# GpSimd's two-tensor operations in pieces of 256 columns, and a modulation stage that starts nine feeds later

## The chip, the cores and the metric

The kernel runs on one core of a Trainium2 chip. The metric is the device time of one execution in microseconds (us), lower is better. TensorE (PE) multiplies, VectorE (DVE) and ScalarE (ACT) do elementwise work, GpSimd (POOL) does elementwise work in SBUF and issues the indirect DMAs, and SyncE (SP) issues nearly all other DMAs.

## The reference

The program computes three transformer layers on 1024 tokens of width 1024, in float32. What matters here is the first layer's modulation and attention, and the three output projections:

```python
mod = jax.nn.silu(c) @ w_ada[l] + b_ada[l]                 # 6 vectors of 1024
shift1, scale1, gate1, shift2, scale2, gate2 = jnp.split(mod, 6, axis=-1)
h = rms_norm(x, norm1_g[l]) * (1.0 + scale1) + shift1      # needs 2 of the 6
mla_out = mla_attention(...)                               # 4 heads, softmax
d_out = diff_attention(...)                                # 4 heads, softmax1 - lam * softmax2
d_out = rms_norm(d_out, subln_g[l]) * (1.0 - lambda_init)
mix = jnp.concatenate([mla_out, d_out], axis=-1) @ w_out[l]
x = x + gate1 * mix                                        # the other 4 come here and later
```

After it come a mixture of 32 experts, a layer with causal attention over 16 heads, and a layer with a window of 128 tokens over 16 heads; each of the two attention layers ends in an output projection of its own.

## The kernel before

The order of the work is written out by hand. Each engine runs its own instructions strictly in program order. The program order comes from generators: a unit of work is a Python generator, a `Pipe` (L70) holds the active ones, and each call of `go.feed` (L77) lets every active unit emit its instructions up to its next `yield`, in the order in which the units were added. One such call is a **feed**. A unit given to `spawn` begins with the next feed.

**Products in float32.** Every weight and activation is split into a high part and a rest (`split`, L332): the high part is a rounded copy, the rest is a subtraction. On the usual path ACT makes the copy and DVE the subtraction; with `e=G` GpSimd makes both (L338, L339) on tiles of 128x1024.

**Attention of the first layer** (`phase_attn`, L966) goes in 35 **rounds** of three feeds, counted from 0 (L1152): feed one adds a unit of the latent attention (`m_unit`, ten matmuls of 512 columns at L1079), feeds two and three add a unit of the differential attention each (`d_unit`, matmuls at L1116 and L1117, four of either a round). The latent units run three rounds behind (LAG = 3), so the first three rounds have no `m_unit`. In each round one `d_unit` ends on DVE with L1137 to L1140: L1138 is a tiny operation, L1139 adds the two softmax tiles of 128x1024, both with two inputs in SBUF, and TensorE's transposes at L1006 wait for L1139. Every second round a `d_end` (L1038) normalises one 256-column piece of the output: `rstd_of` (L319) is a DVE step (L321) and a power on GpSimd (L322); three feeds later L1054 and two L1056 on DVE use it, and TensorE's transposes at L1060 wait for these.

**The rest of the modulation** (`ada_rest`, L595) runs beside this attention, spawned just ahead of its first round (L1150). It goes 32 times over a piece of `w_ada`, 8 pieces for each of the four remaining vectors: SP loads the next piece (L581, 512 KB, a ring of two buffers, so the load waits until the sum that read the buffer is done), GpSimd scales the present one (L616) and adds it to the accumulator (L617), both 128x1024. The next iteration comes two or three feeds later, in turn. After eight, `finish` waits four feeds, lets TensorE sum over the partitions (L591), and SP writes the vector out (L608).

**Output weights** (`OutWeights`, L923): for the first layer GpSimd multiplies the four raw tiles of each half by the gate vector (`scale`, L932: four instructions of 128x1024) in rounds 30 and 34, and splits the first half in rounds 31 and 32 (`WO_ATTN`, L52, counted from `LAG`). The later layers give four and eight splits to GpSimd (`WO_FOX`, `WO_SWA`).

Of the kernel before, what the change touches and what calls it, by code (L numbers as in the profile page):

```python
# [14 lines left out]
OP = mybir.AluOpType  # L15
# [4 lines left out]
P = 128  # L20
S = 1024
D = 1024
# [13 lines left out]
LAG = 3  # L36
# [29 lines left out]
def f(ap):  # L66
    return ap.bitcast(F32)
# [226 lines left out]
def three_layer_kernel(ctx: ExitStack, tc: tile.TileContext, I, out, stop=99, dbg=None):  # L294
    nc = tc.nc
    V, A, G, T, SP = (GUARD(e) for e in (nc.vector, nc.scalar, nc.gpsimd, nc.tensor, nc.sync))
# [16 lines left out]
    def acopy(dst, src, scale=None):  # L313
        if scale is None:
            A.activation(out=dst, in_=src, func=AF.Copy)  # L315
        else:
            A.activation(out=dst, in_=src, func=AF.Copy, scale=scale)  # L317
# [10 lines left out]
    def bc_load(dst, src_row, n):  # L328
        SP.dma_start(out=dst, in_=bass.AP(tensor=src_row.tensor, offset=src_row.offset,
                                          ap=[[0, dst.shape[0]], [1, n]]))  # L330

    def split(hi, lo, src, scale=None, e=V):  # L332

        if scale is None:
            if e is V:
                A.activation(out=hi, in_=src, func=AF.Copy)  # L336
            else:
                e.tensor_copy(hi, src)  # L338
            e.tensor_tensor(lo, src, f(hi), op=OP.subtract)  # L339
        else:  # L340
            A.activation(out=hi, in_=src, func=AF.Copy, scale=scale)  # L341
            V.scalar_tensor_tensor(lo, src, scale, f(hi), op0=OP.mult, op1=OP.subtract)  # L342

    def split_k(hi, lo, raw, gain=None):
        if gain is None:
            split(hi, lo, raw)
        else:
            for k in range(raw.shape[1]):
                split(hi[:, k], lo[:, k], raw[:, k], gain[:, k:k + 1])
# [14 lines left out]
    def transposed(hi, lo, src, ps_ring=None, n=KD):  # L364

        m = src.shape[0]
        for c in range(0, n, 4):
            ps = (ps_ring or p_tr).tile([P, 4, P], name="tr")[:, :, :m]
            for k in range(4):
                T.transpose(ps[:, k], src[:, (c + k) * P:(c + k + 1) * P], ident[:m, :m])  # L370
            split(hi[:, c:c + 4], lo[:, c:c + 4], ps)
# [201 lines left out]
    def ada_acc(j, pl, e):  # L573
        acc = pl.tile([P, D], F32, name="acc", bufs=2)
        e.memset(acc, 0.0)
        SP.dma_start(out=acc[0:1], in_=I["b_ada"][0:1, j * D:(j + 1) * D])
        return acc

    def ada_load(pl, j, k):
        w = pl.tile([P, D], F32, name="adaw")  # L580
        SP.dma_start(out=w, in_=I["w_ada"][0][k * P:(k + 1) * P, j * D:(j + 1) * D])  # L581
        return w
# [4 lines left out]
    def ada_sum(acc, m=P):  # L587
        res = []
        for c in range(2):
            ps = p_tr.tile([P, 512], name="adaps")[0:m]  # L590
            T.matmul(ps, lhsT=ones[:, 0:m], rhs=acc[:, c * 512:(c + 1) * 512], start=True, stop=True)  # L591
            res.append(ps)
        return res

    def ada_rest():  # L595

        ad = Rings(sb, 2)
        todo = [(j, k) for j in range(2, 6) for k in range(KD)]
        w = ada_load(ad, *todo[0])
        accs = {}  # L600

        def finish(j):
            for _ in range(4):
                yield
            for c, ps in enumerate(ada_sum(accs[j], 1)):
                acopy(accs[j][0:1, c * 512:(c + 1) * 512], ps)
            yield
            SP.dma_start(out=d_mod[j:j + 1], in_=accs[j][0:1])  # L608
            if j == 5:
                ad.close()  # L610

        for i, (j, k) in enumerate(todo):
            w2 = ada_load(ad, *todo[i + 1]) if i + 1 < len(todo) else None
            if k == 0:
                accs[j] = ada_acc(j, ad, G)
            G.tensor_scalar(w, w, cc[:, k:k + 1], None, op0=OP.mult)  # L616
            G.tensor_tensor(accs[j], accs[j], w, op=OP.add)  # L617
            w = w2
            for _ in range(2 + i % 2):
                yield  # L620
            if k == KD - 1:
                go.spawn(finish(j))

# [299 lines left out]
    class OutWeights:  # L923
# [5 lines left out]
        def scale(self, c, row):  # L929

            for r in self.raw[c]:
                G.tensor_tensor(r, r, row[:, None, c * 512:(c + 1) * 512].to_broadcast([P, 2, 512]), op=OP.mult)  # L932

        def load(self, c):
            self.raw[c] = [sb.tile([P, 2, 512], F32, f"{self.name}{c}{q}") for q in range(4)]
# [30 lines left out]
    def phase_attn(wo, following):  # L966
# [181 lines left out]
        go.after(start_m)  # L1148
        go.feed()
        go.spawn(ada_rest())  # L1150
        seq = [(h, g, qi) for h in range(4) for g in range(4) for qi in range(2)]
        for i in range(len(seq) + LAG):  # L1152
# [1223 lines left out]
```

## Time and profile before

| | |
|---|---|
| Median of three runs | 2639.68 us |
| Lowest and highest | 2635.43 and 2639.68 us |
| Profiled execution | 2630.55 us |
| Its span, first to last instruction | 2628.8 us |
| Busy share: PE, DVE, ACT, POOL | 94%, 70%, 56%, 20% |
| Mean granted TensorE clock | 0.977 |

The profile comes from one execution of its own. An engine is busy when it executes; of DVE and GpSimd the time that an instruction waits for access to SBUF counts in its duration, so such a wait is seen as an instruction that takes longer than others of its kind. A time in brackets at a row's end is the idle time of the engine ahead of it, with what ended it.

### The profile page before, as it was taken

What the parts mean: (1) busy time and instruction counts of PE and PEld (TensorE: products, weight loads), DVE (VectorE), ACT (ScalarE), POOL (GpSimd) and SP (SyncE); (2) the same over time, 40 slices, a digit from 0 to 9 for tenths busy, and PEclk for the clock granted to TensorE, in tenths of its full rate; (3) what the DMA queues carried; (4) which work ended last, traced back from release to release, by engine and by line L of the source; (5) the groups of instructions that cost most, each with busy time, mean ns of one, the idle gap of its engine ahead of it and who ended that gap; (6) DMA issues with size and microseconds to landing.
All of it is one profiled execution on the core that took longest, in us unless ns stands there. A gap on an engine that the chain in (4) does not pass through costs nothing. (4 is left out here: it accounts for less than half of the span.)

```text
span 2628.8 us, 37168 instructions
## 1 busy us (share of the span) xinstructions
PE 2469.2 (94%) x13658; PEld 2057.6 (78%) x13658; DVE 1828.9 (70%) x3072; ACT 1460.3 (56%) x2557; POOL 529.2 (20%) x355
## 2 busy tenths in 40 slices
PE   5999899898997999999996999999999899999999
PEld 3789777776885777777765887898999789888877
DVE  7654589888667999999998444546888436735952
ACT  3325577676314888888874343446888224436830
POOL 0000276644101222222211012210002002300400
PEclk9999899999997999999998999999999999999999
DMA  7355865352766999999987534437667324337423
GB/s 264 113 143 157 248 199 156 127 156 99 236 223 211 387 387 390 385 379 378 384 300 265 179 112 124 139 105 189 175 167 207 115 87 147 120 108 184 142 70 107
DMA packets 270415, 530.04 MB, mean 202 GB/s; under 512 B 28027, under 2 KB 180603, under 8 KB 244118
## 3 DMA queue, kind: packets, MB, share of 16 engines
q1 hardware_dynamic: 263062, 510.84, 59.2%
q0 software_dynamic: 7168, 16.79, 1.9%
q8 instruction: 109, 1.79, 0.3%
q14 instruction: 76, 0.62, 0.1%
HBM read 424.19 MB, written 111.76 MB: 204 GB/s over the span
## 5 line engine op out<-in xcount | busy, mean ns | idle before, releaser
L358 PE MATMUL ps<-t,t 128*128 128x512 f32 (+5 forms) x8224 | 1760.3, 370 | 3.5 <-DVE t L339 2.6
L358 PEld LDWEIGHTS ps<-t,t 128*128 128x128 f32 (+1 forms) x8224 | 1379.0, 182 | 313.2 <-DVE t L339 4.9
L336 ACT ACTIVATE t<-ps 128x512 fp32r<-128x512 f32 (+3 forms) x660 | 334.8, 545 | 331.2 <-PE ps L370 204.6
L339 DVE TENSOR_TENSOR t<-t,t 128x2048 fp32r<-128x2048 f32 (+4 forms) x226 | 471.5, 2112 | 55.8 <-ACT t L336 55.7
L339 DVE TENSOR_TENSOR t<-ps,t 128x512 fp32r<-128x512 f32 (+3 forms) x660 | 392.1, 623 | 93.3 <-ACT t L336 86.5
L336 ACT ACTIVATE t<-t 128x2048 fp32r<-128x2048 f32 (+4 forms) x226 | 400.0, 1774 | 31.4 <-DVE t L764 10.9
L322 POOL TENSOR_TENSOR small<-small 128x8 f32<-128x8 f32 (+3 forms) x120 | 135.8, 1131 | 1006.9 <-DVE small L321 973.9
L317 ACT ACTIVATE t<-ps,small 96x512 f32<-96x512 f32 (+5 forms) x208 | 128.7, 619 | 335.1 <-PE ps L358 278.3
L315 ACT ACTIVATE t<-ps 128x256 f32<-128x256 f32 (+3 forms) x196 | 88.6, 454 | 133.5 <-PE ps L358 73.1
L370 PE MATMUL ps<-small,t 96*128 96x96 f32 (+1 forms) x736 | 96.0, 271 | 46.8 <-DMA t<-d_x 18.6
L370 PEld LDWEIGHTS ps<-small,t 96*128 96x128 f32 (+1 forms) x736 | 83.8, 147 | 67.6 <-DVE t L1869 19.0
L1501 POOL DMA_INDIRECT d_ye<-t,small x32 | 45.3, 1417 | 436.3 <-ACT t L317 429.7
L2036 DVE CUSTOM_DVE_ANT_0 t<-ps,t 128x1024 f32<-128x1024 f32 (+7 forms) x128 | 95.6, 747 | 20.0 <-PE ps L2031 18.1
L2118 DVE TENSOR_TENSOR t<-t,ps 128x512 f32<-128x512 f32 x32 | 22.0, 688 | 124.4 <-PE ps L358 124.4
L342 DVE SCALAR_TENSOR_TENSOR t<-t,small,t 128x512 fp32r<-128x512 f32 (+5 forms) x124 | 80.2, 692 | 36.1 <-ACT t L341 36.1
L616 POOL TENSOR_SCALAR t<-t,small 128x1024 f32<-128x1024 f32 x32 | 96.7, 3022 | 36.7 <-DMA t<-in_w_ada_dram 36.7
L2040 ACT ACTIVATE t<-t,small 128x1024 f32<-128x1024 f32 (+7 forms) x128 | 99.3, 776 | 7.3 <-DVE small L2036 5.3
L1497 POOL DMA_INDIRECT t<-d_h,small x32 | 89.0, 2781 | 33.7 <-DVE small L1205 24.3
L1698 DVE TENSOR_REDUCE small<-t 128x8 f32<-128x512 f32 (+1 forms) x56 | 36.2, 647 | 79.0 <-ACT t L1697 78.9
L1006 PE MATMUL ps<-small,t 128*128 128x128 f32 x512 | 69.8, 281 | 21.7 <-DVE t L1139 16.4
L1079 PE MATMUL ps<-t,t 128*128 128x512 f32 x320 | 83.8, 408 | 4.9 <-ACT t L1125 4.5
L2055 PE MATMUL ps<-small,t 128*128 128x128 f32 x576 | 85.4, 275 | 1.0 <-ACT t L2040 0.8
(298 smaller groups left out, 3070.3 us busy)
## 6 DMA issues: line engine op xcount, KB each, us to landing
t<-in_w_expert_gate_dram SPq DMA_DIRECT2D x64, 1024.0 KB
t<-in_w_expert_up_dram SPq DMA_DIRECT2D x64, 1024.0 KB
t<-in_w_expert_down_dram SPq DMA_DIRECT2D x64, 1024.0 KB
t<-in_w_ada_dram SPq DMA_DIRECT2D x48, 512.0 KB
t<-d_ak SPq DMA_DIRECT2D x64, 256.0 KB
t<-in_w_in_a_dram SPq DMA_DIRECT2D x12, 1024.0 KB
t<-in_x_dram SPq DMA_DIRECT2D x16, 512.0 KB
t<-d_dk SPq DMA_DIRECT2D x16, 512.0 KB
```

Source lines behind the costliest of these rows:

```text
L315: A.activation(out=dst, in_=src, func=AF.Copy)
L317: A.activation(out=dst, in_=src, func=AF.Copy, scale=scale)
L322: G.tensor_tensor(dst, dst, mhalf[:, :dst.shape[-1]], op=OP.pow)
L336: A.activation(out=hi, in_=src, func=AF.Copy)
L339: e.tensor_tensor(lo, src, f(hi), op=OP.subtract)
L358: T.matmul(ps, lhsT=a(k), rhs=b(k), start=(first and i == 0), stop=(last and i == n - 1))
L370: T.transpose(ps[:, k], src[:, (c + k) * P:(c + k + 1) * P], ident[:m, :m])
L616: G.tensor_scalar(w, w, cc[:, k:k + 1], None, op0=OP.mult)
L1497: G.indirect_dma_start(out=xg[e % 3], out_offset=None, in_=d_h2, in_offset=rows(idx_in[:CAP, e:e + 1]), bounds_check=S - 1, oob_is_err=False)
L2036: V.tensor_tensor_reduce(sbt[:, :n], ps[:, :n], c[:, :n], -1.0, 3e38, OP.add, OP.min, nm)
L2040: A.activation(out=pt[:, :n], in_=sbt[:, :n], func=AF.Exp, scale=-1.0, bias=nm, accum_out=RS[h][:, qt:qt + 1])
L2055: T.transpose(tr[:, j], pt[:, (b + j) * P:(b + j + 1) * P], ident)
```

## The change

A new helper `fine` issues a GpSimd two-tensor operation as pieces of 256 columns. Three places use it: the subtraction of `split` on GpSimd, the sum of `ada_rest`, and the product of `scale`. In `ada_rest` the first feeds change too: the first load is issued as before, both accumulators are reserved at once, and then nine feeds (3 * LAG) pass. In each iteration one feed now lies between scaling and sum, and one behind the sum, so an iteration takes two feeds instead of 2.5 on average. The sums are computed in the same order of pieces as before.

```diff
+    def fine(out, a, b, op):
+
+        for c in range(0, out.shape[-1], 256):
+            G.tensor_tensor(out[:, c:c + 256], a[:, c:c + 256], b[:, c:c + 256], op=op)
+
     def split(hi, lo, src, scale=None, e=V):
 
         if scale is None:
             if e is V:
                 A.activation(out=hi, in_=src, func=AF.Copy)
+                e.tensor_tensor(lo, src, f(hi), op=OP.subtract)
             else:
                 e.tensor_copy(hi, src)
-            e.tensor_tensor(lo, src, f(hi), op=OP.subtract)
+                for k in range(src.shape[1]):
+                    fine(lo[:, k], src[:, k], f(hi[:, k]), OP.subtract)
...
         w = ada_load(ad, *todo[0])
         accs = {}
+        ad.reserve("acc", D, 2)
+        for _ in range(3 * LAG):
+            yield
...
             G.tensor_scalar(w, w, cc[:, k:k + 1], None, op0=OP.mult)
-            G.tensor_tensor(accs[j], accs[j], w, op=OP.add)
+            yield
+            fine(accs[j], accs[j], w, OP.add)
             w = w2
-            for _ in range(2 + i % 2):
-                yield
+            yield
             if k == KD - 1:
                 go.spawn(finish(j))
...
             for r in self.raw[c]:
-                G.tensor_tensor(r, r, row[:, None, c * 512:(c + 1) * 512].to_broadcast([P, 2, 512]), op=OP.mult)
+                for k in range(2):
+                    fine(r[:, k], r[:, k], row[:, c * 512:(c + 1) * 512], OP.mult)
```

## Rows read from the trace of the kernel before

**Rows 1.** Page, part 1: engine, busy us, share of the span, instructions.
```profile
PE 2469.2 (94%) x13658; PEld 2057.6 (78%) x13658; DVE 1828.9 (70%) x3072; ACT 1460.3 (56%) x2557; POOL 529.2 (20%) x355
```
**Rows 2.** Stages: window, length, busy us (instructions) of PE, PEld, DVE, ACT, POOL; clock, DMA.
```profile
328.50:555.00 226.50, 203.27 (x1244) 173.27 (x1242) 200.54 (x291) 164.30 (x316) 153.32 (x67) 0.98 0.59 170
```
**Rows 3.** PE's waits, 328 to 570 us: who for whom, total us, times, longest.
```profile
PE ps L1006 <- DVE t L1139: 12.7, 9, 1.6
PE ps L1060 <- DVE t L1056: 5.5, 5, 1.5
...
PE ps L591 <- DVE t L339: 3.1, 1, 3.1
```
**Rows 4.** Two of DVE's lines over the span: duration ns min/median/max, first and last start.
```profile
L1139 DVE SCALAR_TENSOR_TENSOR t<-t,small,t x32: 1283/1285/3346, 317.5 to 654.0; 128x1024 f32<-128x1024 f32 x32
L1056 DVE TENSOR_SCALAR t<-t,small x32: 274/288/2477, 352.6 to 673.5; 128x128 f32<-128x128 f32 x32
```
**Rows 5.** DVE, in order of time: start us, duration us, instruction.
```profile
403.52 0.17 DVE L321 TENSOR_SCALAR small<-small 128x2 f32<-128x2 f32 x1 [1.14 <-ACT small L1048]
...
407.57 3.34 DVE L1139 SCALAR_TENSOR_TENSOR t<-t,small,t 128x1024 f32<-128x1024 f32 x1
...
413.49 0.15 DVE L1054 TENSOR_TENSOR small<-small 128x2 f32<-128x2 f32 x1
413.68 3.56 DVE L1056 TENSOR_SCALAR t<-t,small 128x128 f32<-128x128 f32 x2
```
**Rows 6.** POOL in order of time, the same stretch as rows 5.
```profile
403.77 0.73 POOL L322 TENSOR_TENSOR small<-small 128x2 f32<-128x2 f32 x1 [5.40 <-DVE small L321]
404.49 2.86 POOL L616 TENSOR_SCALAR t<-t,small 128x1024 f32<-128x1024 f32 x1
407.43 2.40 POOL L617 TENSOR_TENSOR t<-t,t 128x1024 f32<-128x1024 f32 x1
409.81 3.82 POOL L616 TENSOR_SCALAR t<-t,small 128x1024 f32<-128x1024 f32 x1
413.71 2.36 POOL L617 TENSOR_TENSOR t<-t,t 128x1024 f32<-128x1024 f32 x1
416.05 2.85 POOL L616 TENSOR_SCALAR t<-t,small 128x1024 f32<-128x1024 f32 x1
```
**Rows 7.** PE's waits, 604 to 664 us.
```profile
PE ps L1060 <- DVE t L1056: 6.9, 4, 2.6
PE ps L1006 <- DVE small L1140: 4.2, 1, 4.2
```
**Rows 8.** The first scale of the output weights: POOL's four products, DVE's two L1056.
```profile
605.38 9.42 POOL L932 TENSOR_TENSOR t<-t,t 128x1024 f32<-128x1024 f32 x4 [4.15 <-DMA t<-in_w_out_dram]
...
610.26 4.63 DVE L1056 TENSOR_SCALAR t<-t,small 128x128 f32<-128x128 f32 x2
```
**Rows 9.** PE's waits, 2464 to 2497 us, the largest.
```profile
PE ps L2268 <- DVE small L2272: 1.5, 2, 0.7
```
**Rows 10.** GpSimd's smallest two-tensor product, line view: duration ns min/median/max.
```profile
L1882 POOL TENSOR_TENSOR small<-small x8: 194/195/707, 1415.0 to 1464.8; 128x1 f32<-128x1 f32 x8
```
**Rows 11.** PE's groups from 328.5 to 554.9 us: the score matmuls of a round.
```profile
L1116 PE MATMUL ps<-t,t 128*128 128x512 f32 x84 | 36.8, 438 | 0.0
```
**Rows 12.** The first feeds: DMA issues on SP, and ACT's wait, in order of time.
```profile
296.26 1.57 SPq L581 DMA_DIRECT2D t<-in_w_ada_dram  x2
...
298.28 0.53 SPq L893 DMA_DIRECT2D d_mq<-t  x1
...
306.01 1.09 ACT L336 ACTIVATE t<-ps 128x512 fp32r<-128x512 f32 x2 [2.80 <-DMA d_mq<-t]
```
**Rows 13.** POOL's groups from 328.5 to 554.9 us: the clearing of an accumulator.
```profile
L575 POOL MEMSET t<- 128x1024 f32 x3 | 2.9, 955 | 0.0
```
**Rows 14.** POOL's waits, 328 to 570 us.
```profile
POOL small L322 <- DVE small L321: 51.1, 9, 7.9
POOL t L616 <- DMA t<-in_w_ada_dram: 20.5, 5, 7.9
POOL t L617 <- DMA t<-in_b_ada_dram: 5.3, 2, 4.7
```

## The prediction

> **What bounds the kernel now.** The page first: PE is busy for 94% of the span and GpSimd for 20% [rows 1], so time is TensorE's, and the change touches TensorE only where GpSimd holds something up. So the second view is the table of stages, for the stretch of the attention in which the modulation runs: of 226.5 us PE is busy for 203.3, DVE for 200.5, GpSimd for 153.3 [rows 2]. PE loses some 10% there, and DVE is nearly as full as PE. The third view says what ended PE's idle time: 12.7 us for L1139 on DVE, 5.5 for L1056, 3.1 for a split that followed two L1056 [rows 3], 21.3 us together.
>
> Why these are late is seen when DVE and GpSimd are laid side by side. L1139 takes 1.28 us in most cases and 3.35 at worst, L1056 0.28 and 2.48 [rows 4]. At 407.57 L1139 took 3.34 us: it began 0.14 us after a sum of GpSimd (L617, 407.43 to 409.83) and seems to have run when that had ended. At 413.68 two L1056 took 3.56 us: the next sum ran from 413.71 to 416.07 [rows 5, 6]. A DVE operation that reads two tensors, or the fast scaling of L1056, waits for a whole GpSimd sum. The collision comes again and again because one clock drives both: the power at L322 starts 0.25 us after L321, the scaling 0.72 later, the sum 2.94 later, in all 3.91 us behind L321; L1139 comes 4.05 behind it [rows 5, 6].
>
> GpSimd's scaling (L616) does less harm: the second of the two L1056 ended at 417.24, 1.19 us after that scaling began, though it ran for 2.85 [rows 5, 6]; less its own 0.28, the scaling held it for 0.9 us.
>
> The output weights show the same: 6.9 us behind L1056 and 4.2 behind L1139 (the row names its follower L1140) from 604 to 664 us [rows 7], with two L1056 that took 4.63 us beside four products in a row [rows 8]; I take these 11.1 us. In the third layer's attention the largest such wait is 1.5 us [rows 9]. All in all 33.9 us of TensorE's idle time hang on GpSimd.
>
> **The change, part by part.**
>
> *What a piece costs.* No row shows 256 columns. Four products in a row took 9.42 us, 2.355 each for 1024 columns [rows 8]; one column takes 0.195 [rows 10]. A sum of 2.39 (the median of 2.36 to 2.40) less 0.195 over 1023 columns is 2.146 ns a column. Spacing back to back is then 0.157 + 0.00215 n: 0.706 us for 256, 2.82 for four. Ends: 2.355 if the fixed part were hidden wholly, 2.98 (four times 0.195 + 255 x 2.146 ns) if none were. I take 2.82, as the rows at both sizes fix it, so a sum grows by 0.47 us.
>
> The Trainium skill speaks against cutting: "GPSIMD Engine Reference", section 3.1, has 4497 ns for 2048 columns and two dispatch hops in software for each instruction. With the 2.39 us here for 1024 that is an estimate of 2.06 ns a column and 0.76 us a piece, 6 to 7 us more GpSimd time over 128 pieces; the sum below doesn't use it.
>
> *What a collision costs then.* A DVE operation waits for the rest of one piece, 0.7 us at most, in place of 2.1 to 2.2. The next operation can lose one piece again: when one of the four products ends, a waiting DVE operation gets in, and the one behind it meets the next product (two L1056 in 4.63 us beside products 2.355 apart, [rows 8]). PE has some slack: L1139's delay of 2.06 us costs PE 1.6 [rows 3, 4], so 0.5 is absorbed; a pair of L1056 lost 3.0 us (3.56 less twice 0.28), and the five waits of rows 3 are 1.1 each, two to such a pair, so about 0.8 is absorbed [rows 3, 5]. L1138 with L1139 lose two pieces at most and 0.8 us on average, 0.3 after slack; L1054 and two L1056 1.4, 0.6 after slack. GpSimd reads for a sum during 2.82 of some 6.6 us, 43%. The stretch has 21 rounds (84 matmuls at L1116, four a round [rows 11]) and 10 `d_end`: 21 x 0.43 x 0.3 + 10 x 0.43 x 0.6 = 5.3 us; I take 5, with ends of 0 and 12. **Saved: 21.3 - 5 = 16.3 us.**
>
> *Output weights.* The two L1056 with L1054 lose 1.7 in place of 5.7 us; the split rounds keep the copy's hold (1.04 us each, not cut); the second scale's L1138 and L1139 lose 0.9 in place of 2.9. I keep 3.9 of 11.1 us. **Saved 7.2**, ends 4 and 10. Their 0.47 us for each 1024 columns, 12 times, lies beside TensorE's work; the first product with these weights comes long after. *Third layer:* 1.5 us and little beside it; **saved 1**, ends -1 and 2.5 (eight splits grow by 3.8 us, used only in the output projection behind the stage). The second layer's four splits cost no wait that I found: 0.
>
> *The start.* The first load stays; the second load and the bias row leave the queue ahead of `d_mq`'s write (SP, 296.26 to 298.28), for whose landing ACT idled 2.80 us [rows 12]. Of the 2.80 us I give half, as one of two loads goes: **saved 1.3**, ends 0 and 2.8. Two more loads that were queued among the first attention loads go as well; nothing of that is in the sum.
>
> *What the change adds: less room on GpSimd.* Iterations now go every two feeds, 64 feeds from feed 10 to feed 73, which are those 21 rounds. Without the stalls they take 226.5 - 21.3 + 5 = 210 us, 6.57 an iteration. GpSimd needs 2.94 for the scaling, 2.82 for the sum, and 0.37 for eleven powers of 0.73 and four memsets of 0.955 [rows 13]: 6.13. Spare: 0.44 x 32 = 14 us. It is drawn on by DVE operations that get in first (L616 at 3.82 in place of 2.85 is one, 0.97 [rows 6]): 1.5 us per round for L1138 and L1139 in half the rounds, 15 us, ends 6 and 38; and by late loads, 25.8 us in two kinds before, when GpSimd was idle 51.1 us beside [rows 14]; a fuller GpSimd hides most, 9 us, ends 0 and 26. Who waits for a late GpSimd: the power of L322 stands in the same queue, and DVE, in order, stops at L1054 for it, with all the reductions and splits behind. L1054 comes 9.97 us after L321 [rows 5], so the queue may run 9 us late for nothing. Sum: 24 - 14 - 9 = 1; I charge **4**, ends 0 and 41. SP is also held: the load of piece i+1 waits for the sum of i-1, now one feed old in place of two or three, and writes of `d_mix`, the loads of the next q and of the next head stand behind it; q is asked for two rounds ahead, so some us hurt nobody, and it shares those ends.
>
> **Sum:** 16.3 + 7.2 + 1 + 1.3 - 4 = 21.8 us saved. The profiled execution was 2630.55 us (its span and 1.75 us around it), 9.1 below the median of 2639.68: 2608.8 against it, and against the median, which I predict, **2617.9 us**.
>
> **The rivals.**
>
> *GpSimd becomes the bound (slower).* Its queue has 6.13 us of work for 6.57. If DVE gets in ahead of a piece in every round (38 us) and the late loads come back whole (26), it ends 64 - 14 - 9 = 41 us late, all paid at L1054: 41 - 25.8 gained = 15 slower, 2655 us. It costs from 6.85 us an iteration on (9 us over 32), and is slower than before from 6.85 + 25.8/32 = 7.66 on. For: by the code three of the 64 feeds meet the loads of a new head, and rows 14 have a single wait of 7.9 for one. Against: two thirds of GpSimd's idle time before was waiting for DVE's L321 [rows 14]. Near its middle this cancels the gain: no change.
>
> *The pieces go as one train.* If DVE gets in only behind the fourth piece, each collision costs 2.8 in place of 2.36, some 14 big ones, and the start's 1.3 us is all that is won: 2639.7 - 1.3 + 14 x 0.45 less those that move away, about 2641. Against: beside the four products DVE got in between each two [rows 8].
>
> *GpSimd's scaling holds as long as it runs.* It stays whole: with 2.85 us of hold, 44% of 21 rounds and 10 `d_end` lose 0.9 after slack more, 12 us: 2630. Against: the 0.9 us hold above. By "SBUF — State Buffer" of the Trainium skill, section "SBUF: two separate sides", who starts first keeps the shared ports for the whole instruction; the sums here agree (2.1 us of 2.4), L616 doesn't.
>
> **How the numbers follow.** Forecast (2604 to 2632): 0.62. Scaling holds: 0.06, also faster. Train, or a late GpSimd that eats the gain: 0.18, no change. GpSimd the bound: 0.14, slower. 0.2% is about what a measurement of this kernel can tell. For 8 in 10 the range is 2601 (all ends good, 36.6 us, and 2 for the spread of runs) to 2645, which leaves out the worst of the bound.
>
> **What would show it.** Right: pieces 0.7 us apart; L1139 at most 2.0 us and L1056 at most 1.0 in the attention; PE's waits for L1139 and L1056 under 8 us from round 3 on; the 3.1 us at L591 gone; the power at L322 never 9 us behind L321. Wrong: DVE waits for GpSimd at L1054; pieces over 0.85 us apart; L1139 still over 3 us; `d_mq`'s landing still waited for as long. What would make it wrong altogether is a full GpSimd queue that holds SP and so the loads of a head.

## The result, and the profile after

The changed kernel takes 2598.28 us (median of four runs, 2596.69 to 2603.41) against 2638.06 for the kernel before (2635.43 to 2639.68): ratio 0.9854, interval 0.9843 to 0.9866. On another chip it took 2599.60 (2597.74 to 2604.15) against 2637.89. The gain is 38 to 40 us; the forecast was 21.8 us and 2617.9, with 2601 as the low end of its range, so the time lies below the range. (The forecast counts from 2639.68, the median of the first three runs of before.) The profiled execution took 2597.42 us (span 2595.7, granted clock 0.977).

The numbers of lines have moved: L1116 is now L1127, L1079 L1090, L1125 L1136, L1139 L1150, L1140 L1151, L1054 L1065, L1056 L1067, L1006 L1017, L1060 L1071, L591 L598, L616 L626, L339 L342, L358 L365, and all pieces stand at L335. Experiments are quoted with their own numbers: E1 two and E4 three lower than after, E5 the same, E7's third layer two to five higher; E8 is cut from before and stands one lower than that.

Page, part 1, of after (columns as in [rows 1]):

```profile
PE 2461.7 (95%) x13658; PEld 2053.3 (79%) x13658; DVE 1798.1 (69%) x3072; ACT 1458.0 (56%) x2557; POOL 557.7 (21%) x523
```

GpSimd has 28.5 us more of work in 168 more instructions; DVE, with the same 3072, is busy for 30.8 us less. That is waiting for GpSimd that no longer counts as work.

Stages of after (columns as in [rows 2]): the start, the stretch of [rows 2], its continuation up to the output weights, and the two halves of the output weights; then the start and the same two halves in before:

```profile
302.00:325.50 23.50, 13.05 (x52) 9.61 (x51) 14.72 (x26) 11.48 (x20) 0.84 (x1) 0.78 0.99 290
325.50:539.00 213.50, 202.10 (x1244) 171.65 (x1242) 187.96 (x293) 165.69 (x318) 189.77 (x167) 0.99 0.62 181
539.00:587.80 48.80, 48.07 (x301) 41.46 (x302) 39.83 (x67) 38.12 (x78) 14.86 (x16) 1.00 0.45 162
587.80:607.20 19.40, 19.07 (x124) 16.68 (x122) 17.45 (x29) 15.72 (x31) 12.47 (x16) 1.00 0.12 35
607.20:632.90 25.70, 22.00 (x140) 18.70 (x139) 21.06 (x35) 17.26 (x34) 21.92 (x28) 1.00 0.28 99
```
```profile
303.60:328.50 24.90, 14.86 (x53) 10.28 (x52) 14.73 (x26) 11.62 (x20) 15.41 (x6) 0.73 1.02 321
606.80:632.60 25.80, 20.37 (x124) 17.80 (x122) 22.61 (x29) 15.80 (x31) 15.02 (x9) 0.93 0.18 60
632.60:664.70 32.10, 25.06 (x140) 22.00 (x139) 24.80 (x35) 16.81 (x33) 18.98 (x10) 0.84 0.21 75
```

The same 1244 matmuls take 213.5 us in place of 226.5, with GpSimd busy for 89% of the time. In the output weights look at the clock beside PE's busy time: 140 matmuls were busy for 25.06 us at a mean clock of 0.84 and are busy for 22.00 at 1.00. So less idle time is only part of the gain; the work itself has become shorter.

PE's waits in after, 325.5 to 560 us (as [rows 3]), then the lines of [rows 4]:

```profile
PE ps L1090 <- ACT t L1136: 5.7, 8, 2.1
PE ps L1071 <- DVE t L1067: 1.6, 3, 0.8
PE ps L1017 <- DVE t L1150: 1.4, 4, 0.4
PE ps L1127 <- DMA t<-d_dq: 1.3, 1, 1.3
PE ps L598 <- DVE t L342: 0.9, 1, 0.9
```
```profile
L1150 DVE SCALAR_TENSOR_TENSOR t<-t,small,t x32: 1283/1672/2116, 314.8 to 624.6; 128x1024 f32<-128x1024 f32 x32
L1067 DVE TENSOR_SCALAR t<-t,small x32: 273/638/1166, 346.3 to 641.7; 128x128 f32<-128x128 f32 x32
```

The 21.3 us of [rows 3] are down to 3.9. Collisions have become more frequent and smaller: L1150's median rose from 1285 to 1672 ns while its maximum fell from 3346 to 2116.

GpSimd in order of time (as [rows 6]), and its waits, 325.5 to 560 us (as [rows 14]):

```profile
398.15 2.84 POOL L626 TENSOR_SCALAR t<-t,small 128x1024 f32<-128x1024 f32 x1
400.96 0.73 POOL L322 TENSOR_TENSOR small<-small 128x2 f32<-128x2 f32 x1
401.66 3.80 POOL L335 TENSOR_TENSOR t<-t,t 128x256 f32<-128x256 f32 x4
405.44 2.89 POOL L626 TENSOR_SCALAR t<-t,small 128x1024 f32<-128x1024 f32 x1
408.42 2.83 POOL L335 TENSOR_TENSOR t<-t,t 128x256 f32<-128x256 f32 x4
```
```profile
POOL t L335 <- DMA t<-in_b_ada_dram: 23.3, 1, 23.3
POOL t L626 <- DMA t<-in_w_ada_dram: 21.3, 5, 7.0
POOL small L322 <- DVE small L321: 1.3, 1, 1.3
```

Four pieces take 2.82 us, or 3.80 when a DVE operation gets in between; the power at L322 goes through at once. Of the 51.1 us that GpSimd waited for L321 [rows 14] 1.3 are left. The 23.3 us ended at 326.17, so nearly all of them lie ahead of these rounds; what is left of GpSimd's idle time there is the waiting for loads (21.3).

### The profile page after: what moved, and what is told of

Same layout as the page of the kernel before. It is cut to its first block, busy times and chain, and to the rows that moved or that the text cites. A ratio compares the mean times of both kernels' runs of the same rounds, so it can differ in the third digit from the quotient of the medians.

```text
span 2595.7 us, 37353 instructions
## 1 busy us (share of the span) xinstructions
PE 2461.7 (95%) x13658; PEld 2053.3 (79%) x13658; DVE 1798.1 (69%) x3072; ACT 1458.0 (56%) x2557; POOL 557.7 (21%) x523
## 5 line engine op out<-in xcount | busy, mean ns | idle before, releaser
L365 PE MATMUL ps<-t,t 128*128 128x512 f32 (+5 forms) x8224 | 1758.3, 370 | 3.8 <-DVE t L342 2.4
L365 PEld LDWEIGHTS ps<-t,t 128*128 128x128 f32 (+1 forms) x8224 | 1377.0, 182 | 313.0 <-DVE t L342 4.4
L342 DVE TENSOR_TENSOR t<-t,t 128x2048 fp32r<-128x2048 f32 (+4 forms) x226 | 472.3, 2115 | 55.3 <-ACT t L341 55.2
L342 DVE TENSOR_TENSOR t<-ps,t 128x512 fp32r<-128x512 f32 (+3 forms) x660 | 391.8, 623 | 89.7 <-ACT t L341 83.2
L322 POOL TENSOR_TENSOR small<-small 128x8 f32<-128x8 f32 (+3 forms) x120 | 137.3, 1145 | 944.8 <-DVE small L321 912.2
L335 POOL TENSOR_TENSOR t<-t,t 128x256 f32<-128x256 f32 (+1 forms) x224 | 166.3, 774 | 27.1 <-DMA t<-in_b_ada_dram 23.3
L315 ACT ACTIVATE t<-ps 128x256 f32<-128x256 f32 (+4 forms) x196 | 88.4, 453 | 125.0 <-PE ps L365 69.9
L2047 DVE CUSTOM_DVE_ANT_0 t<-ps,t 128x1024 f32<-128x1024 f32 (+7 forms) x128 | 95.5, 747 | 19.5 <-PE ps L2042 17.6
L626 POOL TENSOR_SCALAR t<-t,small 128x1024 f32<-128x1024 f32 x32 | 92.6, 2894 | 31.9 <-DMA t<-in_w_ada_dram 31.9
L1090 PE MATMUL ps<-t,t 128*128 128x512 f32 x320 | 83.6, 408 | 8.1 <-ACT t L1136 7.6
L2066 PE MATMUL ps<-small,t 128*128 128x128 f32 x576 | 86.2, 277 | 0.4 <-ACT t L2051 0.3
## 6 DMA issues: line engine op xcount, KB each, us to landing
t<-in_w_expert_down_dram SPq DMA_DIRECT2D x64, 1024.0 KB, 10.5
```

The lines of the kernel that those rows point to most:

```text
L322: G.tensor_tensor(dst, dst, mhalf[:, :dst.shape[-1]], op=OP.pow)
L335: G.tensor_tensor(out[:, c:c + 256], a[:, c:c + 256], b[:, c:c + 256], op=op)
L365: T.matmul(ps, lhsT=a(k), rhs=b(k), start=(first and i == 0), stop=(last and i == n - 1))
L2047: V.tensor_tensor_reduce(sbt[:, :n], ps[:, :n], c[:, :n], -1.0, 3e38, OP.add, OP.min, nm)
```

## The experiments

Two theories were set against each other: that whole GpSimd sums hold DVE up, so that the pieces bring the gain, and with it the granted clock, which the forecast had left out; or that the new start and pace of the modulation bring it. The table has for each kernel the stage's length, TensorE's idle time in it and the time at a granted clock of 0.5, all in us, worked out from the profiles; stages are cut at the same matmul in each kernel and named by their times in the kernel before.

```
                      328.5-555 (rounds 3-24)  606.8-632.6     632.6-664.7     2440-2525 (third layer)
before                226.5  23.2   6.8    25.8  5.4  3.4   32.2  7.0 10.2   85.0  4.8  6.8
after                 213.5  11.4   3.4    19.3  0.3  0.0   25.8  3.7  0.0   79.4  2.8  0.0
E1 whole, new pace    218.2  14.2  10.2    21.1  0.8  3.4   32.5  7.1 10.2   85.0  6.1  3.4
E2 pieces, old pace   208.1   8.2   0.0    20.1  0.9  0.0   25.7  3.7  0.0   79.5  2.9  0.1
E3 weights only       226.5  25.6   0.0    20.2  0.9  0.0   26.5  3.3  3.4   79.4  2.9  0.0
E4 no nine feeds      230.8  24.5  17.1    19.3  0.3  0.0   25.8  3.7  0.0   79.5  2.9  0.0
E5 pieces of 512      219.1  15.6   6.8    21.0  1.9  0.0   29.9  5.5  6.8   85.0  6.3  1.3
E5 pieces of 128      227.9  25.0   5.1    18.8  0.2  0.0   24.0  2.7  0.0   79.8  3.2  0.0
E7 six stalls         214.2  12.2   3.4    19.3  0.3  0.0   25.8  3.7  0.0   87.9  6.8  9.4
E8 no sums            202.5   4.6   0.0    25.9  5.5  3.4   32.2  7.1 10.2   84.9  4.7  6.8
B1 old pace, 6 feeds  207.0   5.7   3.4    21.3  0.3  0.0   26.6  3.3  3.4   79.5  2.9  0.0
```

**E1: the new start and pace, GpSimd's operations whole.** From after:

```diff
-            fine(accs[j], accs[j], w, OP.add)
+            G.tensor_tensor(accs[j], accs[j], w, op=OP.add)
...
-                for k in range(2):
-                    fine(r[:, k], r[:, k], row[:, c * 512:(c + 1) * 512], OP.mult)
+                G.tensor_tensor(r, r, row[:, None, c * 512:(c + 1) * 512].to_broadcast([P, 2, 512]), op=OP.mult)
```

(The subtraction of `split` is made whole too.)

> The changed kernel with its nine feeds and its two feeds an iteration, but every GpSimd operation whole again (128x1024). Theory (the size of a piece does it: a DVE operation waits for a whole GpSimd operation, TensorE idles and its granted clock falls for some us after): the collisions are back, with only the start's 1.4 us and some luck of alignment left, so 2620 to 2640 us, L1150 (L1139 before) up to 3.3 us, half-clock stretches in the output-weight rounds and in the third layer's attention as before. Rival (the new pace and the late start do it, by moving GpSimd's work away from DVE's): 2612 us or less.

Measured: 2619.92 us (2615.47 to 2620.46), ratio 0.9912 (0.9895 to 0.9928). Without pieces 22 of the 40 us are lost again, 12.3 of them in the second half of the output weights and the third layer, which stand as before. What I had no price for is the other half: rounds 3 to 24 gain 8.3 us and the first half of the output weights 4.7 although nothing is cut. TensorE's largest wait, 325 to 560 us:

```profile
PE ps L1015 <- DVE t L1148: 6.9, 6, 2.4
```

A sum still holds L1148 for as long as before (3.33 us at most), but TensorE waits for it six times in place of nine [rows 3]. The sum now stands a feed behind its scaling and all of it starts nine feeds later; which of the two does it was not separated.

**E2: pieces everywhere, the old start and pace.** From before: the three uses of `fine`, nothing else.

> The kernel before with all three places in pieces, but the modulation as before: no nine feeds, scaling and sum in one feed, 2 or 3 feeds an iteration. Theory (piece size): all but the start's 1.4 us comes, 2598 to 2606 us. Rival (pace): the 13 us of rounds 3 to 24 stay out, 2610 us or more.

Measured: 2599.39 us (2591.24 to 2600.14), ratio 0.9829 (0.9808 to 0.985). Pieces alone bring as much as the whole change. Pace and pieces are two cures for the same collisions, and their gains (22 and 43 us in this comparison) don't add up.

**E3: pieces in the output weights and splits only.** From before: `fine` in `split` and `scale`; the sums of the modulation stay whole.

> The kernel before with pieces in the output weights alone (scale and split), the modulation's sums whole. Theory: 11 to 12 us less in the rounds that scale and split the first layer's weights and 6 us less in the third layer's attention, of which the idle time of TensorE is about 8 and 2.5 and the rest the granted clock that no longer falls there; 2616 to 2624 us. Rival (only idle time counts, as in the prediction's sum): 7 and 1 us less, 2628 to 2632 us.

Measured: 2621.27 us (2617.43 to 2626.64), ratio 0.9929 (0.9911 to 0.9947). The output weights go from 58.0 to 46.7 us and the third layer from 85.0 to 79.4, rounds 3 to 24 stay at 226.5: 16.9 us, where the prediction's terms for them were 7.2 and 1. TensorE's idle time there fell by 10.1 us and its time at half clock by 17.0, so idle time alone leaves 6.8 us open.

**E4: after without the nine feeds.**

```diff
-        ad.reserve("acc", D, 2)
-        for _ in range(3 * LAG):
-            yield
```

> The changed kernel without the nine feeds at the start of the modulation's rest; pieces and two feeds an iteration stay. Theory: 1 to 3 us slower than the changed kernel (the write of d_mq lands later again at the start), 2599 to 2602 us. Rival (the late start carries a good part): 2606 us or more.

Measured: 2618.64 us (2615.33 to 2621.47), ratio 0.9912 (0.9895 to 0.993): 20 us slower than after, where I expected 1 to 3. The waits of DVE, 325 to 560 us, and in order of time the first two of them:

```profile
DVE small L1062 <- POOL small L322: 14.2, 3, 7.0
```
```profile
355.98 1.08 DVE L1062 TENSOR_TENSOR small<-small 128x2 f32<-128x2 f32 x1 [7.02 <-POOL small L322]
...
403.30 1.08 DVE L1062 TENSOR_TENSOR small<-small 128x2 f32<-128x2 f32 x1 [3.63 <-POOL small L322]
```

This is the prediction's slower rival, live: with two feeds an iteration GpSimd runs late, its power at L322 began up to 14.2 us behind L321's end, DVE stops at L1062 with all its splits behind, and TensorE pays 11.3 us for L1064. In after the power is 5.7 us late at most and DVE never waits. So the nine feeds are what makes the two-feed pace bearable.

**E5: pieces of 512 and of 128 columns.** From after, 256 in `fine` replaced.

> The changed kernel with pieces of 512 columns. Theory (a DVE operation waits for the rest of one piece; what is over TensorE's slack of 0.5 us costs, and a long enough idle time also costs clock): a piece lasts 1.29 us, so L1150 is at most 1.28 + 1.2 = 2.5 us, TensorE idles some 5 us more in rounds 3 to 24 and some 3 us more with the output weights; GpSimd has 0.3 us less per sum. 2602 to 2612 us. Rival (GpSimd's total time decides, so longer pieces are better): below 2596 us.

> The changed kernel with pieces of 128 columns. By the piece's price (0.697 us for 256 columns, 2.355 for 1024, so 0.145 + 0.00216 n) a sum takes 8 x 0.42 = 3.37 us, 0.6 more than in pieces of 256, and GpSimd needs 6.7 us an iteration. Theory: waits per collision are shorter, but GpSimd, which was up to 5.7 us late at the power of d_end, gets 10 us and more late in the cycles that meet the loads of a new head, and DVE waits at L1065 for it (slack 9 us): 2602 to 2620 us, with DVE's wait for L322 visible. Rival (only the wait per collision counts): 2590 to 2597 us.

Measured: 2614.21 us (2613.52 to 2620.02), ratio 0.9893 (0.9876 to 0.9909), with 512, 2 us above what I expected; 2615.90 (2614.98 to 2617.63), ratio 0.9902 (0.9885 to 0.9918), with 128. The two lose for opposite reasons. PE's waits, 325 to 560 us, with 512:

```profile
PE ps L1017 <- DVE t L1150: 6.0, 6, 1.5
```

and DVE's and PE's with 128:

```profile
DVE small L1065 <- POOL small L322: 5.2, 3, 2.3
```
```profile
PE ps L1127 <- DMA t<-d_dq: 8.9, 3, 3.9
PE ps L1071 <- DVE t L1067: 8.8, 7, 1.8
```

SP's wait with 128, ahead of the load of the next piece (L588), behind which the loads of q (L387) stand; in after it is 140.6 us and 8.0 at most:

```profile
SPq L588 <- POOL t L335: 157.7, 30, 9.6
```

With 512 the old collisions are back and the third layer is as long as with whole operations. With 128 the output weights and the third layer, where GpSimd has room, are as good as with 256; in rounds 3 to 24 GpSimd is late, DVE waits for the power, and SP, which waits longer for GpSimd's sums to free a buffer, issues the loads of q late. That last is what the prediction called the thing that could go wrong altogether.

**E7: six stalls in the third layer's attention of after.** Six times, two DVE additions of 128x2048 stand ahead of a unit's reductions; they took 2.28 to 2.29 us each, a little more than the 2.11 expected:

```diff
+                if g < 2 and i in (1, 4, 7) and c == 0:
+                    for _ in range(2):
+                        V.tensor_tensor(idle, idle, idle, op=OP.add)
```

> The changed kernel with two additions of 128x2048 on DVE (2.11 us each) ahead of the reductions of six units of the third layer's attention, far apart, where GpSimd is idle: six stalls of 4.2 us that have nothing to do with GpSimd. Theory (a stall costs TensorE its idle time and then a stretch at 1.2 GHz): 6 x 3.7 = 22 us of idle time and 10 to 20 us of clock, so 32 to 42 us slower than the changed kernel. Rival (idle time alone): 20 to 25 us slower.

Measured: 2638.80 us (2632.68 to 2643.78, ten runs), 39 to 41 us above after, ratio to before 0.9992 (0.9976 to 1.0007). The first pair on DVE, and the largest of PE's waits, 2130 to 2520 us:

```profile
2376.39 4.61 DVE L2285 TENSOR_TENSOR t<-t 128x2048 f32<-128x2048 f32 x2
PE ps L2281 <- DVE small L2288: 23.7, 9, 3.9
```

In the two stages that hold the stalls (329.1 to 357.6 us, and 79.4 to 87.9) TensorE's idle time rises by 21.5 us and the time at half clock by 39.1. In 30.0 of the 39.1 TensorE was busy, which is 15.0 us of lost work; together 36.5 for 37.0 us measured. (Half of the whole 39.1 would be 19.6, which is too much: half clock counts only where TensorE works.) So 21.5 of the 37.0 us are the idle time, and the rest comes after it.

**E8: before without the sum over the eight pieces.**

```diff
-            G.tensor_tensor(accs[j], accs[j], w, op=OP.add)
```

> The kernel before without the sum over the eight pieces of the four modulation vectors; the scaling, the loads and the output weights stay as before. Theory: GpSimd's whole sums cause the 21.3 us of TensorE's idle time in rounds 3 to 24, and the half clock that follows some of it; without them that stretch goes from 226.5 to 202 to 208 us, with no wait over 0.5 us for the sum of the softmax tiles, and the time is 2615 to 2623 us; the output weights and the third layer stay at 58 and 85 us. Rival: what holds DVE is the scaling or something else, and the stretch stays over 215 us and the time over 2627.

Measured: 2605.11 us (2602.84 to 2608.43), ratio 0.9883 (0.9867 to 0.9899). Rounds 3 to 24 take 202.5 us and have 4.6 of idle time, inside what was expected. PE's waits for the softmax sum, 325 to 560 us:

```profile
PE ps L1005 <- DVE t L1138: 1.4, 4, 0.9
```

The longest is 0.9 us, over the 0.5 expected. Output weights and third layer are as before. So the sums caused the stall, the scaling beside them did little harm, and 24.0 us is the most that curing the sums can bring there (E8 also gives GpSimd the time of the sums back); E2 has 18.4 of it, B1 19.5, after 13.0. The whole time is 10 us below the expected 2615: 3.3 of it are the stage behind round 24, which I hadn't counted, and most of the rest is the distance between the profiled execution of before and its timed ones, of which more below: E8 is 27.7 us faster by the profiled executions and 32.8 by the medians.

**B1: pieces, the old pace of 2.5 feeds, a delay of six feeds.** From after:

```diff
-        for _ in range(3 * LAG):
+        for _ in range(6):
...
-            yield
             fine(accs[j], accs[j], w, OP.add)
             w = w2
-            yield
+            for _ in range(2 + i % 2):
+                yield
```

> Pieces of 256 columns in all three places, the modulation in its old pace (scaling and sum in one feed, an iteration every 2 or 3 feeds), begun six feeds later (nine leave no room for its buffers). Theory (the late start is worth some 2 us at the start and keeps GpSimd from being late at the first powers; the old pace leaves GpSimd idle time that the pace of two feeds uses up): rounds 3 to 24 in 207 to 210 us and the start as in the changed kernel, 2590 to 2597 us, better than the changed kernel. Rival (the pace of two feeds is part of the gain): 2600 us or more.

Measured: 2594.82 us (2593.13 to 2596.73), ratio 0.9823 (0.9806 to 0.9839). Then B1 and after side by side on one chip:

> Pieces, the old pace of 2.5 feeds an iteration, the modulation six feeds later: 2592 to 2597 us again, 2 to 7 us below the changed kernel on the same chip. Rival: within 1.5 us of it.

> The changed kernel once more, beside the version with the old pace and six feeds on the same chip. It should give 2598 us again, within 5. If the pace of two feeds costs what the profiles show (213.5 us from round 3 to 24 against 207.0), it is 2 to 7 us above that version. Rival: the difference of the two medians, 3.5 us, is the scatter of runs, and the two are within 1.5 us of each other.

Measured: 2595.53 us (2592.30 to 2598.84) for B1, 2599.60 (2597.74 to 2604.15) for after. B1 is faster than before by 42 to 47 us; its lead on after, 4.1 us here and 3.5 by the first medians, is the size expected, though the runs of the two overlap. In rounds 3 to 24 it has 5.7 us of idle time against 11.4 at the same 3.4 us of half clock. B1 differs from after in the delay too. The pace alone is what E2 and E4 differ in (both in pieces, both without the delay): there the iteration of two feeds takes rounds 3 to 24 from 208.1 us to 230.8, and the whole 19 us longer. So with pieces the shorter iteration is a loss, and the power at L322 comes up to 14.2 us late by it (8.5 in E2).

## Why the prediction was right in its reasons and wrong in its size

**The step that failed** is the first sum, "33.9 us of TensorE's idle time hang on GpSimd", and every saving taken from it: each counted a stall at its idle time. TensorE's time after the stall was taken to be unchanged, and it isn't. Before, around the second half of the output weights (columns as in [rows 2]; the seventh group is the clock), and TensorE there in order of time:

```profile
632.60:638.50 5.90, 3.56 (x25) 2.94 (x24) 5.68 (x7) 3.08 (x6) 5.74 (x5) 1.00 0.02 6
638.50:641.90 3.40, 3.40 (x13) 3.01 (x14) 3.40 (x6) 2.71 (x4) 2.26 (x1) 0.50 0.18 56
641.90:655.60 13.70, 10.88 (x71) 9.53 (x70) 8.44 (x14) 7.29 (x17) 4.70 (x3) 1.00 0.43 158
655.60:662.40 6.80, 4.92 (x21) 4.49 (x22) 5.90 (x8) 2.29 (x4) 6.28 (x3) 0.50 0.01 2
```
```profile
652.38 0.87 PE L358 MATMUL ps<-t,t 128*128 128x256 f32 x6
657.48 1.94 PE L1006 MATMUL ps<-small,t 128*128 128x128 f32 x8 [4.23 <-DVE small L1140]
659.26 2.59 PE L358 MATMUL ps<-t,t 128*128 128x256 f32 x9
```

TensorE stood still for 4.23 us; within that gap the granted clock fell to 0.50, which is 1.2 in place of 2.4 GHz, and stayed there up to 662.40. Nine matmuls of L358 took 2.59 us; in after, at 1.00, the same nine:

```profile
619.46 1.32 PE L365 MATMUL ps<-t,t 128*128 128x256 f32 x9
```

The wait of 4.23 us thus cost a second time. Working with the table's columns, where half of the half-clock time is lost work as far as TensorE was busy in it:

- *Rounds 3 to 24* with the stage behind them: the prediction had 16.3 - 4 = 12.3 us. Idle time fell by 14.2, half clock by 3.4 (1.7 lost), and the two stages by 15.9. The stalls of [rows 3] fell by 17.4, near the 16.3; the charge for GpSimd's fullness is about 3 us (17.4 less 14.2), seen as `L1090 <- ACT L1136` (5.7 us, 3.5 before) and the wait for d_dq (1.3, none before). Term and charge were right.
- *Output weights*: 7.2 predicted; idle time fell by 8.4, half clock by 13.6, with TensorE busy in 11.4 of it (4.92 of the last 6.80 us above; 5.7 lost): 12.9 us shorter. The idle term was right, the clock was missing.
- *Third layer*: 1 predicted; idle time 2.0, half clock 6.8 (3.4 lost): 5.6 shorter. Here waits of 1.5 us [rows 9] looked too small to matter, and most of the gain is clock. Part of the stage before and after (194 and 201 matmuls):

```profile
2464.00:2497.00 33.00, 30.31 (x194) 26.82 (x194) 32.52 (x98) 24.90 (x86) 26.94 (x16) 0.90 0.36 132
```
```profile
2436.80:2464.80 28.00, 27.34 (x201) 24.63 (x200) 27.52 (x99) 25.71 (x91) 26.23 (x35) 1.00 0.40 142
```

- *The start*: 1.3 predicted, 1.4 measured, though not by idle time (10.0 before, 10.5 after); half clock fell by 3.4, with TensorE busy for 9.0 us of it before and 5.4 after (1.8 lost). The split is a matter of the execution: the profile of after's second measurement has the same 23.5 us with 9.2 of idle time and 13.7 at half clock. ACT's waits on d_mq fell from 4.8 to 3.0 us, so the landing is still waited for, but not for as long.

Together the touched stages are 35.8 us shorter, against 21.8 predicted: 24.1 of idle time, foreseen at 21.8, and 12.7 of clock, foreseen at nothing (1.0 too much together). Stages that the change doesn't touch gave some 3 us back (700 to 790 us in before: 90.0, the same matmuls in after 92.3, with 5.0 us more at half clock), so the profiled executions differ by 33.1.

**The second failed step** is the transfer to the median: "9.1 below the median" was carried over as if it were a constant. After's profiled execution lies 0.9 below its median. Of the 19.6 us by which the forecast missed, 8.2 are this, and the other 11.4 the terms above. Much of it goes with the clock again. Of 29 timed executions of before, 27 had mean clocks of 0.970 to 0.975 and took 2633.8 to 2645.9 us; two had 0.977 and 0.979 and took 2629.8 and 2630.4, like the profiled one (0.977, 2630.55). That one was a lucky draw; in the twelve other profiles of this record the profiled execution lies between 3.8 us below its median and 5.8 above. The mean clock of the 29 is 0.9730 and of after's eight 0.9768; 0.0038 of 2638 is 10 us if TensorE was busy in all of it, and 6 by the 29 themselves, among which 0.001 more of clock goes with 1.6 us less. With 25 us less idle time in the profiles that makes 31 to 35 of the 40 between the means (2639.7 and 2599.7); the other 5 to 9 stay open, as the idle time of the executions without a profile isn't seen.

**What held.** Pieces stand 0.70 us apart (predicted 0.706). The estimate by the Trainium skill, "GPSIMD Engine Reference", section 3.1, was too high here: 0.76 us as the prediction has it, and 0.81 as its two figures give it (2.39 less 768 columns at 2.06 ns). Two bounds were missed by little: L1150's maximum is 2.12 us (2.0) and L1067's 1.17 (1.0). The power at L322 is at most 5.7 us late (under 9), the waits for L1150 and L1067 together are 3.0 us from 325.5 to 560 (under 8), the 3.1 at L591 are 0.9. The train of pieces didn't come (of the four pieces at 401.66 that took 3.80 us the third alone took 1.71, beside L1150), nor a scaling that holds for its whole length. One hold hadn't been thought of: L321, a DVE operation on 128x2, took 0.79 us in place of 0.17 [rows 5] where a scaling (POOL, from 416.95 on) had just begun. DVE's next reduction, ACT's L1136 and so TensorE's L1090 stand behind such delays in order; what they cost was not tested:

```profile
417.29 0.79 DVE L321 TENSOR_SCALAR small<-small 128x2 f32<-128x2 f32 x1 [1.13 <-ACT small L1059]
```

**What was mis-seen of the change.** The nine feeds were priced at 1.3 us of the start. By E4 they are worth 20 us at this pace, as without them GpSimd's power is up to 14.2 us late and with them 5.7; why the later start makes it less late was not tested. That it should do so much was nowhere in the prediction, though its rival with a late GpSimd had the mechanism, the place (L1054) and the sign. What start and pace together do with whole operations, 8.3 us in rounds 3 to 24 in E1, wasn't priced either. That after came out near E2, and the charge of 4 us near the 3 measured, is luck: two effects priced at 1.3 and 4 us cancel, 20 us won by the later start (after against E4) and 19 lost by the pace (E4 against E2).

## What to carry to other kernels

When a stall is priced, read the granted clock of the stretch behind it, and add to the idle time half of the half-clock time in which TensorE is busy: in E7 that was 15 us beside 21.5. Give an engine that shares SBUF access with a busier one short operations, and choose the length from both sides: the longest hold that the other engine's consumer can absorb, and the room that the engine has for the fixed cost of more pieces (256 columns beat 512 and 128 by 16 and 18 us here). Where a gain comes from two engines missing each other, price a change of start or pace as a term of its own, and compare the profiled execution's clock with those of the timed ones before a median is forecast from it.

## What the hardware showed that was not expected

- Half a clock followed on small gaps. In the third layer of before TensorE lost 0.48 and 0.75 us behind two DVE operations, 1.4 us apart, and then ran 6.8 us at 0.50 without a gap:

```profile
2476.00:2481.70 5.70, 4.33 (x29) 3.49 (x29) 5.63 (x15) 5.05 (x18) 5.49 (x3) 1.00 0.00 1
2481.70:2488.50 6.80, 6.80 (x28) 6.31 (x29) 6.73 (x17) 2.82 (x9) 6.64 (x5) 0.50 0.00 0
```

- Pieces of 512 columns, 1.3 us each, gave the third layer nothing (85.0 us, as with 1024), pieces of 256 gave all (79.4) and 128 no more (79.8). From one size to the next the cost of a hold there is a step.
- GpSimd's scaling of 128x1024, with one tensor and a column of factors, runs for 2.85 us but held no DVE operation that met nothing else for more than 0.89, in before and in after, and without sums beside it (E8) TensorE's waits for L1138 came to 1.4 us; a DVE operation on 128x2 is held too (0.6 us, above).
